# Low parts of x last in the first products of a sublayer, and three first tiles instead of two at five projections

## The chip, the cores and the metric

The kernel runs on one core of a Trainium2 chip. Its time is the device time of one execution, in microseconds; of several runs the median is taken. TensorE multiplies matrices, VectorE and GpSimd do elementwise work, ScalarE casts, squares and activations, SyncE issues most transfers.

## What is computed

Two blocks of a sequence model with 512 positions and 1024 channels, in fp32. The first has two layers, each of four sublayers, the second block three more:

```python
for l in range(DEPTH):
    x = x + 0.5 * rms_norm(swiglu(rms_norm(x, ln_ffn1_pre[l]), w_ffn1_in[l], w_ffn1_out[l]), ln_ffn1_post[l])
    mix = token_mixing(rms_norm(x, ln_mix_pre[l]), ...)
    x = x + rms_norm(mix, ln_mix_post[l])
    x = x + 0.5 * rms_norm(swiglu(rms_norm(x, ln_ffn2_pre[l]), w_ffn2_in[l], w_ffn2_out[l]), ln_ffn2_post[l])
    gate = jax.nn.sigmoid(rms_norm(x, ln_ple_pre[l]) @ w_ple_gate[l])
    x = x + rms_norm(gate * (p[l] @ w_ple_proj[l]), ln_ple_post[l])
x = x + hybrid_mixer(rmsnorm(x, norm_mix_w), ...)
x = x + memory_cross_attention(rmsnorm(x, norm_xattn_w), ...)
x = x + peer_ffn(rmsnorm(x, norm_ffn_w), ...)
```

So every sublayer norms x, projects it, and (in the first block) norms its result before adding it to x.

## The kernel before, in words

Activations lie with the channels on partitions: x is eight tiles of 128 channels by 512 positions. Every fp32 product is made of three: weights and activations are each split into a high part (rounded to the matmul's input type) and a low part (the rest), and `mm3` (line 196 is the matmul that it issues) adds high by high, weight high by x low, and weight low by x high. In the names of tiles `wh`, `wl` are the parts of a weight, `xh`, `xl` those of x, `st` the weight as loaded. `load_w` casts `st` to `wh` on ScalarE (line 186) and subtracts for `wl` on VectorE (line 187), in the last mixer (`mix2`) on GpSimd. There are three buffers each of `wh` and `wl`, two of `st`.

The norm's weight for a position is not applied to x but to the products: `bcast_R` adds up the squares (line 425), makes a reciprocal root in nine small steps on VectorE (lines 254 and 229 to 236, `rsm`, `rsy`, `rst`) and spreads it by TensorE and ScalarE to the tile R; the evacuations of the products multiply by R.

`lin_fm` makes a projection: for each output tile of 128 channels, three products for each of eight tiles of x. At a passage from one sublayer to the next the work is cut in two halves of 256 positions. The last `tail` output tiles of the old sublayer, and the first `head` tiles of the new one, run half by half. Between them stands `post_half`, once for each half: the old result's column sums (`ysum`, `ylast`, on TensorE into the bank `pr`), the nine steps, the multiply of each of eight tiles by R (line 347), the add of x (line 349 on VectorE for even tiles, line 348 on GpSimd for odd ones), the high part on ScalarE (line 351), the low part on VectorE (line 343), then squares for the new norm (lines 273 and 275). Its VectorE instructions are tied in the order written, and so are ScalarE's.

There are eight such passages: ffn to mixer, mixer to ffn, ffn to ple in both layers, ple to the next ffn, ple to the last mixer. The last mixer's output projection (`wdo`), the attention's two (`wxq`, `wxo`) and the last sublayer's (`wpq`) have heads without such a passage ahead; the first sublayer's x is split by `start`.

A scheduler orders each engine's queue ahead of time; `post_half`'s nine steps have a raised priority. Eight PSUM banks are named by use (`banks`); `hd` is the list for head tiles where one is given, otherwise the `ps` list.

## Time and profile before

| | us |
|---|---|
| median of 3 runs | 4402.1 |
| lowest, highest run | 4399.16, 4411.26 |
| profiled execution, its own time | 4405.5 |
| its span in the trace | 4403.7 |
| TensorE busy in it | 4137.3 |
| VectorE busy in it | 2627.9 |

The span runs from the first to the last instruction of the execution; what lies around it is the 1.8 us between the two. A busy TensorE is not TensorE at its peak, since its instructions overlap; where its pitch matters, the starts of its instructions are compared. The mean granted clock of the execution was 0.964 of 2.4 GHz.

### The profile page before, as it was taken

The numbers are of one execution on the slowest core, as the hardware profiler recorded it, in microseconds if no ns is written. First come the engines' busy times: TensorE is split into PE (matmuls) and PEld (weight loads), VectorE is DVE, ScalarE is ACT, GpSimd is POOL, SyncE is SP. The second block draws the span as 40 slices with busy tenths as digits, with TensorE's granted clock in tenths as the row PEclk, the third lists the DMA queues.
The fourth block names the chain that finished last, engine by engine and source line by source line (L and its number), as shares of the span: only waits on it lengthen the run. The fifth ranks groups of instructions, "written<-read, shape, count | busy, mean of one in ns | idle before, by whom it ended". The sixth has DMA issues, their size and how long they took to land. (4 is left out here: it accounts for less than half of the span.)

```text
span 4403.7 us, 56669 instructions
## 1 busy us (share of the span) xinstructions
PE 4137.3 (94%) x21835; PEld 3513.9 (80%) x21835; DVE 2627.9 (60%) x4873; ACT 1609.7 (37%) x2522; POOL 852.8 (19%) x755
## 2 busy tenths in 40 slices
PE   8999999999999999999999889899887889999998
PEld 7887687888888876878888677788777878888887
DVE  5435555643564345656434666636667878777876
ACT  3223423422443234324323543433334743333332
POOL 0002210100110012111001242104564124333331
PEclk9999989999999998989999899999898999999999
DMA  3233101323332341003223311435345689889985
GB/s 126 98 94 123 48 15 48 120 99 96 121 120 96 96 135 44 25 30 120 96 97 124 108 53 34 143 107 178 135 149 182 253 323 334 303 312 318 317 311 183
DMA packets 234815, 629.18 MB, mean 143 GB/s; under 512 B 26800, under 2 KB 93488, under 8 KB 230192
## 3 DMA queue, kind: packets, MB, share of 16 engines
q1 hardware_dynamic: 195232, 464.58, 30.8%
q0 software_dynamic: 38736, 159.93, 10.1%
q8 instruction: 171, 2.80, 0.2%
q10 hardware_dynamic: 576, 1.05, 0.1%
q14 instruction: 100, 0.82, 0.1%
HBM read 562.54 MB, written 62.91 MB: 142 GB/s over the span
## 5 line engine op out<-in xcount | busy, mean ns | idle before, releaser
L196 PE MATMUL ps_ps<-xh,wl 128*128 128x512 f32 (+2 forms) x3568 | 1307.3, 367 | 53.6 <-DVE wl L187 53.6
L196 PE MATMUL ps_ps<-xh,wh 128*128 128x512 f32 (+2 forms) x3568 | 1306.7, 368 | 32.6 <-ACT wh L186 11.9
L196 PE MATMUL ps_ps<-xl,wh 128*128 128x512 f32 (+2 forms) x3568 | 1314.2, 369 | 24.2 <-DVE xl L343 23.8
L186 ACT CAST wh<-st 128x1024 fp32r<-128x1024 f32 (+1 forms) x560 | 580.0, 1038 | 1405.2 <-PE ps_ps L196 962.3
L187 DVE TENSOR_TENSOR wl<-st,wh 128x1024 fp32r<-128x1024 f32 (+1 forms) x496 | 607.2, 1225 | 440.4 <-ACT wh L186 439.3
L196 PEld LDWEIGHTS ps_ps<-xh,wl 128*128 128x128 f32 x3568 | 689.0, 193 | 146.9 <-DVE wl L187 59.9
L196 PEld LDWEIGHTS ps_ps<-xl,wh 128*128 128x128 f32 x3568 | 688.1, 193 | 116.1 <-DVE xl L343 35.2
L196 PEld LDWEIGHTS ps_ps<-xh,wh 128*128 128x128 f32 x3568 | 686.4, 193 | 117.9 <-ACT wh L186 13.4
L442 DVE TENSOR_TENSOR gu<-ps_ps,R 128x512 f32<-128x512 f32 x176 | 121.0, 691 | 447.6 <-PE ps_ps L196 446.8
L348 POOL TENSOR_TENSOR y<-y,x 128x256 f32<-128x256 f32 x64 | 54.8, 856 | 1693.7 <-DVE y L347 1511.6
L196 PE MATMUL ps_ps<-mh,wl 128*128 128x512 f32 (+1 forms) x920 | 327.8, 356 | 2.5 <-DVE wl L187 2.5
L196 PE MATMUL ps_po<-vh,ah 128*128 128x512 f32 x768 | 303.2, 397 | 28.6 <-ACT ah L1845 21.8
L196 PE MATMUL ps_ps<-mh,wh 128*128 128x512 f32 (+1 forms) x920 | 327.4, 356 | 1.2 <-DVE kf L1518 0.9
L196 PE MATMUL ps_po<-vh,al 128*128 128x512 f32 x768 | 304.6, 397 | 4.5 <-DVE al L1846 4.4
L196 PE MATMUL ps_po<-vl,ah 128*128 128x512 f32 x768 | 303.2, 395 | 0.4 <-DVE vl L1852 0.4
L196 PE MATMUL ps_ps<-ml,wh 128*128 128x512 f32 (+1 forms) x792 | 289.4, 365 | 0.0
L187 POOL TENSOR_TENSOR wl<-st,wh 128x1024 fp32r<-128x1024 f32 x64 | 155.9, 2437 | 248.3 <-ACT wh L186 226.2
L1786 POOL DMA_INDIRECT rows<-in_pv_dram,idx x128 | 174.8, 1366 | 121.8 <-DVE acc L1809 114.1
L196 PEld LDWEIGHTS ps_ps<-mh,wl 128*128 128x128 f32 x920 | 174.9, 190 | 26.7 <-DVE wl L187 2.7
L196 PEld LDWEIGHTS ps_po<-vh,ah 128*128 128x128 f32 x768 | 146.4, 191 | 62.0 <-ACT ah L1845 26.2
L196 PEld LDWEIGHTS ps_ps<-mh,wh 128*128 128x128 f32 x920 | 174.8, 190 | 25.7 <-DVE kf L1518 1.1
L196 PEld LDWEIGHTS ps_po<-vh,al 128*128 128x128 f32 x768 | 146.1, 190 | 41.9 <-DVE al L1846 11.6
(699 smaller groups left out, 6047.2 us busy)
## 6 DMA issues: line engine op xcount, KB each, us to landing
st<-in_pu_dram SPq DMA_DIRECT2D x128, 512.0 KB
vst<-in_pv_dram SPq DMA_DIRECT2D x128, 512.0 KB
st<-in_w1i_dram SPq DMA_DIRECT2D x88, 512.0 KB
st<-in_w2i_dram SPq DMA_DIRECT2D x88, 512.0 KB
G<-gst POOLq DMA_DIRECT2D x12, 2048.0 KB
gt<-G SPq DMA_DIRECT2D x384, 64.0 KB
st<-in_wmf_dram SPq DMA_DIRECT2D x44, 512.0 KB
xd<-y SPq DMA_DIRECT2D x20, 1024.0 KB
```

The costliest lines, as they stand in the source:

```text
L186: nc.scalar.copy(out=wh[:, :n], in_=st[:, :n])
L187: self.wl_eng.tensor_sub(wl[:, :n], st[:, :n], wh[:, :n].bitcast(F32))
L196: i = self.nc.tensor.matmul(out, lhsT=lhsT, rhs=rhs, start=start, stop=stop)
L348: nc.gpsimd.tensor_add(y[k + 1], y[k + 1], self.xin[k + 1][:, c])
L442: nc.vector.tensor_mul(t, psum, R)
L1786: self.nc.gpsimd.indirect_dma_start(out=t, out_offset=None, in_=self.d["pur" if w == "u" else "pvr"], in_offset=bass.IndirectOffsetOnAxis( ...
```

## The change

Three things are changed. In `lin_fm` the head's products of a half are issued in three sweeps: all high by high, then all weight low by x high, then all weight high by x low; for `wdo` and `wxo` (`lows=False`) the three stay together for each tile of x, with the x low product last. In `post_half` two multiplies by R become one of 2 x 256 columns, and the eight low parts are issued behind all multiplies and adds. And five projections have three head tiles instead of two: the mixers' `wmf` (twice), the last mixer's `wdf`, and `wdo`, `wxq`, `wxo`. The banks are dealt out to match: a third bank for heads is taken from the attention's list in the mixers and from the gates' list in the last mixer, whose gates are now made with the third tile's evacuation instead of the first's.

```diff
@@ -343,17 +343,14 @@
             dve.append(nc.vector.scalar_tensor_tensor(l[:, c], y[k], self.v(next_gain, k), h[:, c].bitcast(F32), op0=ALU.mult, op1=ALU.subtract))
 
         for k in range(0, KD, 2):
-            for j in (k, k + 1):
-                dve.append(nc.vector.tensor_mul(y[j], y[j], R))
+            pair = self.yh[k // 4][:, k % 4:k % 4 + 2, c]
+            dve.append(nc.vector.tensor_mul(pair, pair, bc(R.unsqueeze(1), [P, 2, T // 2])))
             nc.gpsimd.tensor_add(y[k + 1], y[k + 1], self.xin[k + 1][:, c])
             dve.append(nc.vector.tensor_add(y[k], y[k], self.xin[k][:, c]))
             for j in (k, k + 1):
                 act.append(nc.scalar.activation(self.xs[j][0][:, c], y[j], AF.Copy, scale=self.v(next_gain, j)))
-            if k:
-                lo(k - 2)
-                lo(k - 1)
-        lo(KD - 2)
-        lo(KD - 1)
+        for k in range(KD):
+            lo(k)
         for i, j in zip(dve[1:], dve):
             self.behind(i, j)
         for i, j in zip(act[1:], act):
@@ -372,7 +369,7 @@
             self.yt = None
 
 
-    def lin_fm(self, wsrc, mts, xs, evac, tag, head=0, between=None, tail=0, done=None, wait=(2, 11)):
+    def lin_fm(self, wsrc, mts, xs, evac, tag, head=0, between=None, tail=0, done=None, wait=(2, 11), lows=True):
 
 
         kt = len(xs)
@@ -382,10 +379,12 @@
             pt = [self.ps([P, T], "hd" if "hd" in self.bank else tag) for _ in range(head)]
             ws = [load(m)[0] for m in mts[:head]]
             for c in HALVES:
-                for k in range(kt):
+
+                parts = ((0, 0), (1, 0), (0, 1))
+                steps = [(k, p) for p in parts for k in range(kt)] if lows else [(k, p) for k in range(kt) for p in parts]
+                for n, (k, (a, b)) in enumerate(steps):
                     for j in range(head):
-                        wh, wl, _, _ = ws[j]
-                        self.mm3(pt[j][:, c], (wh[:, k, :], wl[:, k, :]), (xs[k][0][:, c], xs[k][1][:, c]), k == 0, k == kt - 1)
+                        self.mm(pt[j][:, c], ws[j][a][:, k, :], xs[k][b][:, c], n == 0, n == len(steps) - 1)
             self.store_x()
             if between:
                 between()
@@ -552,7 +551,7 @@
         nc, tc, d = self.nc, self.tc, self.d
         with tc.tile_pool(name="mix", bufs=1, reuse_waits="tile") as pool:
             self.tags = {n: ("ax", AXB) for n in "rtab qk vat mq og".split()}
-            self.banks(ps=(0, 1), rw=(2, 3, 4), at=(5, 6, 7), pr=(6, 7))
+            self.banks(ps=(0, 1), rw=(2, 3, 4), at=(6, 7, 5), pr=(6, 7), hd=(0, 1, 5))
             self.pool, self.l = pool, l
             self.C = pool.tile([P, NC1], F32, name="C")
             nc.sync.dma_start(out=self.C, in_=d["C"])
@@ -587,7 +586,7 @@
                     for _ in range(2):
                         next(chain, None)
 
-            self.lin_fm(lambda m: [(d["wmf"][l][m], 0, KD)], list(range(16, 22)) + list(range(16)), self.xs, evac, "ps", head=2)
+            self.lin_fm(lambda m: [(d["wmf"][l][m], 0, KD)], list(range(16, 22)) + list(range(16)), self.xs, evac, "ps", head=3)
             for _ in att:
                 pass
             for _ in chain:
@@ -1196,7 +1195,7 @@
         nc, tc, d = self.nc, self.tc, self.d
         with tc.tile_pool(name="mx2", bufs=1, reuse_waits="tile") as pool:
             self.tags = {}
-            self.banks(ps=(0, 1), gi=(2, 3, 4), gn=(5,), gc=(6, 7), pr=(6, 7))
+            self.banks(ps=(0, 1), gi=(2, 3, 4), gn=(5,), gc=(6, 7), pr=(6, 7), hd=(0, 1, 4))
             self.pool = pool
             self.C = pool.tile([P, NC2], F32, name="C2")
             nc.sync.dma_start(out=self.C, in_=d["C2"])
@@ -1216,7 +1215,7 @@
                 nonlocal chain
                 if m < 12:
                     self.gd_tile(m, psum)
-                    if m == 0:
+                    if m == 2:
                         self.gd_gates()
                     if m == 11:
                         self.gd_core()
@@ -1231,7 +1230,7 @@
                         next(chain, None)
 
             self.wl_eng = nc.gpsimd
-            self.lin_fm(lambda m: [(d["wdf"][m], 0, KD)], list(range(24)), self.xs, evac, "ps", head=2)
+            self.lin_fm(lambda m: [(d["wdf"][m], 0, KD)], list(range(24)), self.xs, evac, "ps", head=3)
             self.wl_eng = nc.vector
             ys = []
             for q in range(2):
@@ -1244,7 +1243,8 @@
             for h in range(4):
                 self.split(self.gd[f"yg{h}"], *ys[4 + h])
             self.res_begin()
-            self.lin_fm(lambda m: [(d["wdo"][m], 0, KD)], list(range(KD)), ys, self.res_tile, "ps", head=2)
+            self.banks(ps=range(5), pr=(5, 6, 7))
+            self.lin_fm(lambda m: [(d["wdo"][m], 0, KD)], list(range(KD)), ys, self.res_tile, "ps", head=3, lows=False)
             self.res_end(next_gain)
 
     def lam_neg(self):
@@ -1558,7 +1558,7 @@
                 if m % 4 == 3:
                     scores(m // 4)
 
-            self.lin_fm(lambda m: [(d["wxq"][m], 0, KD)], list(range(KD)), self.xs, evac, "ps", head=2)
+            self.lin_fm(lambda m: [(d["wxq"][m], 0, KD)], list(range(KD)), self.xs, evac, "ps", head=3)
             ys = []
             for q in range(2):
                 h, lo = self.half(F32R, "ymh"), self.half(F32R, "yml")
@@ -1569,7 +1569,7 @@
                     self.mm(po, vt[:, kk, m * P:(m + 1) * P], pT[m // 2][:, kk, :], kk == 0, kk == 1)
                 self.split(po, *ys[m])
             self.res_begin()
-            self.lin_fm(lambda m: [(d["wxo"][m], 0, KD)], list(range(KD)), ys, self.res_tile, "ps", head=2)
+            self.lin_fm(lambda m: [(d["wxo"][m], 0, KD)], list(range(KD)), ys, self.res_tile, "ps", head=3, lows=False)
             self.res_end(next_gain)
 
 
```

Three places in the queues. VectorE at the first passage into a mixer, before: the second half of the nine steps of the second half's R, with what stands between and behind them up to the first multiply by R. `id` is a constant's cast, `ssum` an add of squares.

```order
L343 SCALAR_TENSOR_TENSOR xl<-y,V,xh 128x256
L234 SCALAR_TENSOR_TENSOR rst<-rsy 128x2
L343 SCALAR_TENSOR_TENSOR xl<-y,V,xh 128x256
L235 TENSOR_TENSOR rst<-rst,rsm 128x2
L343 SCALAR_TENSOR_TENSOR xl<-y,V,xh 128x256
L236 SCALAR_TENSOR_TENSOR rsy<-rst,rsy 128x2
L343 SCALAR_TENSOR_TENSOR xl<-y,V,xh 128x256
L275 TENSOR_TENSOR ssum_2632<-ssum_2632,sqx 128x256
L616 CAST id_2877<-io 128x128
L275 TENSOR_TENSOR ssum_2632<-ssum_2632,sqx 128x256
L347 TENSOR_TENSOR y<-y,ps_pr 128x256
```

And in the changed kernel, from the first half's low parts on, to the sixth of the nine steps (`wgl` is a gate weight's low part, line numbers behind line 349 are one lower or more):

```order
L343 SCALAR_TENSOR_TENSOR xl<-y,V,xh 128x256 x7
L254 TENSOR_SCALAR rsm<-ps_pr 128x2
L343 SCALAR_TENSOR_TENSOR xl<-y,V,xh 128x256
L229 TENSOR_SCALAR rsy<-rsm 128x2
L275 TENSOR_TENSOR ssum_2632<-ssum_2632,sqx 128x256
L230 TENSOR_TENSOR rst<-rsy 128x2
L187 TENSOR_TENSOR wl<-st,wh 128x1024
L231 TENSOR_TENSOR rst<-rst,rsm 128x2
L275 TENSOR_TENSOR ssum_2632<-ssum_2632,sqx 128x256
L232 SCALAR_TENSOR_TENSOR rst<-rst 128x2
L218 TENSOR_TENSOR wgl<-wg,wgh 128x64
L233 SCALAR_TENSOR_TENSOR rsy<-rst,rsy 128x2
```

All but one of the first half's low parts stand ahead of the first step, and a weight cast stands among the steps; before, the low parts stood between the steps.

TensorE at the same passage, before: the head's tenth to twelfth product of the first half, the column sums of the old result's second half, and the next products.

```order
L196 MATMUL ps_ps<-xh,wh 128x256
L196 MATMUL ps_ps<-xl,wh 128x256
L196 MATMUL ps_ps<-xh,wl 128x256
L196 MATMUL ps_pr<-io,ylast 128x1
L196 MATMUL ps_pr<-io,ysum 128x1
L196 MATMUL ps_pr<-io,ylast 128x1
L196 MATMUL ps_ps<-xh,wh 128x256 x2
L196 MATMUL ps_ps<-xl,wh 128x256
```

The changed kernel, from the head's first product on (`hd` is the bank list of heads):

```order
L196 MATMUL ps_hd<-xh,wh 128x256 x16
L196 MATMUL ps_hd<-xh,wl 128x256 x8
L196 MATMUL ps_pr<-io,ylast 128x1
L196 MATMUL ps_pr<-io,ysum 128x1
L196 MATMUL ps_pr<-io,ylast 128x1
L196 MATMUL ps_hd<-xh,wl 128x256 x8
L196 MATMUL ps_hd<-xl,wh 128x256 x3
L196 MATMUL ps_hd<-xh,wh 128x256 x8
L196 MATMUL ps_hd<-xl,wh 128x256 x3
L196 MATMUL ps_hd<-xh,wl 128x256 x8
L196 MATMUL ps_hd<-xl,wh 128x256 x2
L196 MATMUL ps_pr<-io,rsy 128x128 x2
```

The low parts of x come up first behind 32 products, the third tile's high products stand among theirs, and the column sums stand behind 24 products that need high parts alone; before, they stood behind twelve, four of which need a low part.

VectorE at the passage from ple into the last mixer, before: the end of the first half, with the evacuations of the old sublayer's last tiles (`gt`, `prj`) and the first step of the second half's R.

```order
L343 SCALAR_TENSOR_TENSOR xl<-y,V,xh 128x256 x2
L275 TENSOR_TENSOR ssum_18698<-ssum_18698,sqx 128x256
L343 SCALAR_TENSOR_TENSOR xl<-y,V,xh 128x256
L275 TENSOR_TENSOR ssum_18698<-ssum_18698,sqx 128x256
L343 SCALAR_TENSOR_TENSOR xl<-y,V,xh 128x256
L275 TENSOR_TENSOR ssum_18698<-ssum_18698,sqx 128x256
L486 TENSOR_TENSOR gt<-ps_ps,R 128x256
L489 TENSOR_TENSOR prj_18170<-prj_18170,gt 128x256
L486 TENSOR_TENSOR gt<-ps_ps,R 128x256
L322 TENSOR_TENSOR ysum<-ysum,sqy 128x256
L489 TENSOR_TENSOR prj_18171<-prj_18171,gt 128x256
L254 TENSOR_SCALAR rsm<-ps_pr 128x2
```

The changed kernel:

```order
L343 SCALAR_TENSOR_TENSOR xl<-y,V,xh 128x256 x8
L275 TENSOR_TENSOR ssum_18690<-ssum_18690,sqx 128x256 x2
L485 TENSOR_TENSOR gt<-ps_ps,R 128x256
L275 TENSOR_TENSOR ssum_18690<-ssum_18690,sqx 128x256
L488 TENSOR_TENSOR prj_18162<-prj_18162,gt 128x256
L485 TENSOR_TENSOR gt<-ps_ps,R 128x256
L322 TENSOR_TENSOR ysum<-ysum,sqy 128x256
L488 TENSOR_TENSOR prj_18163<-prj_18163,gt 128x256
L254 TENSOR_SCALAR rsm<-ps_pr 128x2
```

The evacuations and the step stand behind all eight low parts, as before; what stood between the low parts stands behind them.

## Rows read from the trace of the kernel before

**Rows 1.** Page: busy time by engine, and TensorE's busy tenths in 40 slices.
```profile
PE 4137.3 (94%) x21835; PEld 3513.9 (80%) x21835; DVE 2627.9 (60%) x4873; ACT 1609.7 (37%) x2522; POOL 852.8 (19%) x755
...
PE   8999999999999999999999889899887889999998
```
**Rows 2.** Windows of three passages: busy us of each engine, granted clock, DMA.
```profile
core 0: us, PE busy (x) PEld busy (x) DVE busy (x) ACT busy (x) POOL busy (x), PEclk, DMA share, GB/s
386.00:408.00 22.00, 17.48 (x109) 14.76 (x110) 20.86 (x52) 12.95 (x33) 13.06 (x16) 0.92 0.47 176
1233.30:1268.00 34.70, 26.65 (x176) 23.82 (x174) 28.14 (x70) 16.96 (x42) 10.90 (x13) 0.90 0.24 93
2468.40:2516.00 47.60, 33.01 (x156) 26.31 (x156) 37.89 (x85) 23.08 (x53) 23.09 (x21) 0.68 0.31 114
```
**Rows 3.** Waits of TensorE: us in total, times, longest.
```profile
PE ps_ps L196 <- DVE wl L187: 61.5, 17, 6.8
...
PE ps_ps L196 <- DVE xl L343: 23.8, 38, 2.4
```
**Rows 4.** Timeline of VectorE, first passage into a mixer: start, us, line, tiles.
```profile
384.33 1.76 DVE L187 TENSOR_TENSOR wl<-st,wh 128x1024 fp32r<-128x1024 f32 x1
...
393.24 0.68 DVE L236 SCALAR_TENSOR_TENSOR rsy<-rst,rsy 128x2 f32<-128x2 f32 x1
393.84 0.47 DVE L343 SCALAR_TENSOR_TENSOR xl<-y,V,xh 128x256 fp32r<-128x256 f32 x1
...
395.30 0.42 DVE L347 TENSOR_TENSOR y<-y,ps_pr 128x256 f32<-128x256 f32 x1 [0.18 <-PE ps_pr L196]
...
402.99 2.98 DVE L343 SCALAR_TENSOR_TENSOR xl<-y,V,xh 128x256 fp32r<-128x256 f32 x4
```
**Rows 5.** Timeline of VectorE, from ple into the last mixer.
```profile
2476.29 3.43 DVE L343 SCALAR_TENSOR_TENSOR xl<-y,V,xh 128x256 fp32r<-128x256 f32 x2
...
2488.09 0.16 DVE L254 TENSOR_SCALAR rsm<-ps_pr 128x2 f32<-128x2 f32 x1 [3.17 <-PE ps_pr L196]
...
2491.68 0.75 DVE L347 TENSOR_TENSOR y<-y,ps_pr 128x256 f32<-128x256 f32 x2 [1.38 <-PE ps_pr L196]
...
2492.69 0.75 DVE L347 TENSOR_TENSOR y<-y,ps_pr 128x256 f32<-128x256 f32 x2
...
2514.80 0.69 DVE L1262 TENSOR_TENSOR cx<-ps_ps,R 128x512 f32<-128x512 f32 x1 [2.87 <-ACT R L428]
```
**Rows 6.** Page: weight casts and low parts of weights; busy, mean ns of one.
```profile
L186 ACT CAST wh<-st 128x1024 fp32r<-128x1024 f32 (+1 forms) x560 | 580.0, 1038 | 1405.2 <-PE ps_ps L196 962.3
L187 DVE TENSOR_TENSOR wl<-st,wh 128x1024 fp32r<-128x1024 f32 (+1 forms) x496 | 607.2, 1225 | 440.4 <-ACT wh L186 439.3
...
L187 POOL TENSOR_TENSOR wl<-st,wh 128x1024 fp32r<-128x1024 f32 x64 | 155.9, 2437 | 248.3 <-ACT wh L186 226.2
```
**Rows 7.** Timeline of TensorE: head's last product and third tile's first, attention.
```profile
2893.95 0.28 PE L196 MATMUL ps_ps<-xh,wl 128*128 128x256 f32 x1
2894.07 0.40 PE L196 MATMUL ps_ps<-xh,wh 128*128 128x512 f32 x1
2894.30 0.40 PE L196 MATMUL ps_ps<-xl,wh 128*128 128x512 f32 x1
```
**Rows 8.** Timeline of TensorE: four waits, in brackets, at three passages and the start.
```profile
23.91 1.05 PE L196 MATMUL ps_pr<-io,ssum 128*128 128x1 f32 x8 [2.75 <-DVE ssum L425]
...
411.46 1.02 PE L196 MATMUL ps_pr<-io,ssum 128*128 128x1 f32 x8 [1.19 <-DVE ssum L425]
...
1267.90 0.79 PE L196 MATMUL ps_ps<-xh,wh 128*128 128x512 f32 x1 [0.30 <-ACT wh L186]
...
2494.26 0.80 PE L196 MATMUL ps_ps<-xh,wh 128*128 128x256 f32 x2 [2.61 <-ACT xh L351]
```
**Rows 9.** Timeline of VectorE: second half's first multiply or step, other passages.
```profile
801.02 0.75 DVE L347 TENSOR_TENSOR y<-y,ps_pr 128x256 f32<-128x256 f32 x2 [0.87 <-PE ps_pr L196]
...
1172.82 0.41 DVE L347 TENSOR_TENSOR y<-y,ps_pr 128x256 f32<-128x256 f32 x1
...
1250.25 0.16 DVE L254 TENSOR_SCALAR rsm<-ps_pr 128x2 f32<-128x2 f32 x1 [2.74 <-PE ps_pr L196]
```

## The prediction

> **What bounds the kernel now.** The page's first part comes first: TensorE is busy 94% of the span, VectorE 60%, and of 40 slices of the span most show TensorE at nine tenths or more [rows 1]. So over most of the kernel only TensorE time counts, and an edit can win only where TensorE stands still. The windows show where: at the passage from one sublayer to the next. In the 22 us around the first passage into a mixer TensorE is busy 17.48 us and VectorE 20.86; in the 47.6 us into the last mixer 33.01 and 37.89, at a mean granted clock of 0.68 of 2.4 GHz, that is, much of it at the lower level, 1.2 GHz [rows 2]. There, and only there, VectorE is the bound. The waits say for what TensorE stood: 23.8 us in 38 waits for the low part of x (line 343), 61.5 us in 17 for low parts of weights (line 187) [rows 3]. The last is the largest, and the change removes none of its causes.
>
> A passage has two halves of 256 columns. In each VectorE multiplies eight tiles by R and adds x, ScalarE makes the high parts, VectorE the low parts; the second half's R waits for the sum of squares of the last tile, made by nine small steps on VectorE. The kernel before puts the low parts between the sums, so a head product waits for a low part almost at once, while later high parts wait behind earlier low parts.
>
> **Part by part.** *The merged multiply.* Two multiplies by R in a row are 0.75 us [rows 4]; one of 512 columns from the same kind of operands took 0.69 [rows 5]. 0.06 x 4 pairs x 2 halves is 0.5 us a passage on VectorE, 4 us over the eight passages, and it is contained in the replays below.
>
> *The order of one half.* Sums of two tiles took 1.01 us, from 2491.68 to 2492.69 [rows 5]; 0.06 less, four times, is 3.8 us. Eight low parts at 0.47 each, undisturbed [rows 4], are as much. At the first passage into a mixer the second half's first multiply begins at 395.30 and the last four low parts at 402.99 for 2.98 us, so 10.7 us in all [rows 4]. I take 8.7 for the new order: 7.6 and 1.1 of stretching, since the adds of squares on GpSimd still run beside the low parts (the row with two low parts in 3.43 us beside a weight cast on GpSimd shows the worst of it [rows 5]; four in 2.98 the usual). The high parts of all tiles are there 5.5 us after the first multiply instead of about 8.5, and TensorE then has 48 products per three tiles that need no low part.
>
> *The price: the second half's R.* The nine steps stood between the first half's low parts, one by one. By the order above seven low parts now stand ahead of the first step, and a weight cast, two adds and small casts between the others. Replay: a weight cast on VectorE begins at 384.33 and took 1.76 us, 1.23 where nothing disturbs it [rows 4, 6]; two multiplies, three adds and two small steps behind it, 2.3 us, end the first half's sums at about 388.0; seven low parts bring 391.3, the nine steps at 0.2 are 1.8, what stands between them 2.8: 396.2. Before, the last step began at 393.24 and took 0.68 [rows 4], so 393.9. That half starts 2.3 us later: its first multiply at 397.1, its last low part at 405.8, against 406.0 before. VectorE ends the passage where it did.
>
> *Into the mixers of the two layers (2 passages).* Before, only some nine products of two tiles are left at the last low part, 406.0, 1.0 us of work. After, the 24 products with low parts begin when the 48 others are done, at about 405.9, and take 2.9 us; with the sums of squares between them 409.8, 2.8 us later than before, but with a third tile done in it: 48 products of 256 columns, 0.12 us apart, are 5.76 us, and the tile is then saved further on, at 24 products 0.23 us apart (two rows show each pitch [rows 7]), 5.45 us. The squares are added up earlier, which takes away most of the 1.19 us wait at 411.46 [rows 8]. 5.45 - 2.8 + 1.2 and up to 3 from an earlier R for the mixer's first tiles: I take 5 each (2 to 7), so 10 in both.
>
> *From mixer to ffn (2) and from ple to ffn (1).* Heads were three already. The second half's column sums stand behind first-half products on TensorE that waited for low parts; now these need high parts only, so R comes sooner: at the second its first step waited 2.74 us for TensorE, at 1250.25 [rows 9]. Replay: first multiply 1.9 us earlier than 801.02 in the first case, last low part 2.7 earlier, of which TensorE keeps 1.7, since the weight cast behind three tiles, 0.30 us of waiting before [rows 8], grows by 0.4: all products with the high weight now end last. Sum 3.5 for two (0 to 6). From ple the same gives 3 us earlier and 2.5 kept (0 to 4).
>
> *From ffn to ple (2).* The nine steps again fall behind seven low parts, and behind a weight cast and another; R comes 3.4 us later than the multiply at 1172.82 [rows 9] allowed, the shorter half gives 3 back. Sum 0 (-4 to 4 for two).
>
> *From ple to the last mixer (1).* The worst passage. Its second half's first step is at 2488.09, its first multiply at 2491.68 [rows 5], and TensorE waits 2.61 us for the high part up to 2494.26 [rows 8]. In the first half two low parts took 3.43 us beside a GpSimd weight cast [rows 5]; TensorE went at the half clock through products that low parts fed one by one. Replay: high parts 4 us earlier, first step at 2483, first multiply at 2486.5, heads (three now) done at 2502.4, the mixer's R first used at 2503.1 against 2514.80 [rows 5]. VectorE, which evacuates these tiles, is then 11.7 us earlier; TensorE gains the third tile's 5.45 besides, but waits for the evacuations. I take 11.5 (5 to 15).
>
> *Start (1).* The column sums of the first norm are asked of TensorE behind 55 products, not 73, and come from VectorE no sooner: it waited 2.75 us at 23.91 [rows 8], and 18 products at 0.12, 2.2 us, are now left behind that wait. -1.5 (-3 to 0).
>
> *The three other projections with a third tile.* Three weight buffers are then all in use. Before, the third weight was ready: at 2894.07 the third tile follows the second at pitch [rows 7]. After, the fourth tile's casts wait for the heads' last products: 1.04 us on ScalarE and 1.23 on VectorE [rows 6], of which three evacuations on other engines hide nothing; the third tile at half width costs 0.3 more. The row at 1267.90, where heads were already three, shows 0.30 us for the first cast [rows 8], because the first buffer comes free earlier than the last. Between 0.3 and 2.6: I take 1.7 for the two of the attention, and 1 for the mixer's output, where the products wait for the mixer itself. -4.4 (-7 to -1).
>
> Sum: 10 + 3.5 + 2.5 + 0 + 11.5 - 1.5 - 4.4 = 21.6 us. The profiled run is 4405.5 us, 3.4 above the median of 4402.1; from it 4383.9, from the median 4380.5. I say 4382. The low bounds add up to -5, the high ones to 42: 4407 to 4360.
>
> **A rule that speaks to the order.** Two low parts took 3.43 us in the row above while GpSimd ran a weight cast, and four 2.98 [rows 4, 5]; alone one takes 0.47. The Trainium skill, "GPSIMD Engine Reference", section "1. Specifications", says that GpSimd shares its SBUF interfaces with VectorE and contends with VectorE instructions that have two SBUF inputs. A low part has two such inputs, a multiply by R has one and one in PSUM; by that rule the sums suffer less, and low parts behind GpSimd's adds run alone. The trace agrees on the low parts. What it would be worth is worked out under the rivals.
>
> **Rivals.** *No measurable change.* VectorE is the bound at the passages (20.86 of 22 us [rows 2]) and has 0.5 us less to do in each; a half that ends where it ended and an R that comes later leave only the third tile, and the mixers may be paced by their evacuations so that a tile more at their start is waited away. Then the layers' mixers give 2 each, the last one 5, all else 0 except the losses: 4 + 5 - 5.9 = 3, about 4399. For it: the window's VectorE share. Against it: the slices after the first two passages into a mixer (the fifth to seventh and the sixteenth to eighteenth) have TensorE at nine tenths or more [rows 1].
>
> *Slower.* One mechanism: the three weight buffers. With all three held by heads, the next tile's weight starts at the heads' end, not ahead of it, at six places: two mixers, the last one, its output, two of attention. Each shows 1.04 + 1.23 us on VectorE, in the last mixer 1.04 + 2.44 on GpSimd [rows 6]. 5 x 2.3 + 3.5 is 15; with the 11 that the later R takes at four passages (2 x 2.3 and 2 x 3.4, kept in full) 26, against 12 that then remain of the gains: 4416. It decides if the buffers come free only with the last product of all heads, and the evacuations of three tiles come before the casts. Against it is the 0.30 us row.
>
> *More.* The low parts run alone at 0.47 behind the sums, and the stretches at the lower clock close. The first is 1.1 us x 8 passages, 9; the second, (1 - clock) x window, is 1.8, 3.5 and 15 us for the three windows [rows 2], of which I count 8 as lying beyond the sum. 9 + 8 on top of 21.6: 4364.
>
> That the change does not do what it says is excluded: the order shows each part of it.
>
> **How the numbers follow.** Forecast 4382 (between 4375 and 4389): 0.53. More, 4364: 0.15. No measurable change, 4399: 0.24. Slower, 4416: 0.08. A difference under 0.3%, 13.2 us, is about what a measurement of this kernel cannot tell from none. Faster by more than that (below 4388.9): the first two, 0.68. Within: 0.24. Slower: 0.08. The range leaves out the slower case and the outer half of the larger gain: 4360 to 4403.
>
> **What would show it.** In the profile after: waits of TensorE for the low part of x at line 343 well under 23.8 us; the second half's first multiply about 2 us later at 395 and 1173, earlier at 801, 1253 and by 5 at 2492; eight low parts in about 4.5 us; the last mixer's first evacuation some 11 us earlier; a new wait for the fourth weight of 1 to 2 us in the attention. It would be wrong if the mixers' length from their first evacuation to their end grew by what their start gained, or if the nine steps came later than replayed at the last mixer too.

## The result, and the profile after

The changed kernel took 4438.7 us (median of ten runs, 4424.1 to 4448.3), the kernel before 4402.1: 36.6 us apart; the ratio taken over the ten runs of each is 1.0075, with an interval of 1.0061 to 1.0090. The change made the kernel some 0.8% slower, where 20 us less was forecast. The profiled execution of the changed kernel took 4431.8 us, its span 4429.9; it lies 6.8 below its median, that of before 3.4 above, so the two traces show 26.2 of the 36.6 us.

What the change was to remove is nearly gone. In the page of the changed kernel the group of products with the low part of x (the last columns: idle before it, who ended most of it), and the one wait for it in the heads that have banks of their own (`hd`):

```profile
L196 PE MATMUL ps_ps<-xl,wh 128*128 128x512 f32 (+2 forms) x3456 | 1218.6, 369 | 0.3 <-DVE xl L343 0.3
...
PE ps_hd L196 <- DVE xl L343: 1.8, 1, 1.8
```

The waits of 23.8 us [rows 3] are 2.1. TensorE is also busier where it stood. The windows of the changed kernel over the three passages (the same times as before; columns as in [rows 2]):

```profile
386.00:408.00 22.00, 18.81 (x137) 16.78 (x137) 20.32 (x45) 13.04 (x33) 11.38 (x17) 1.00 0.50 176
1233.30:1268.00 34.70, 28.45 (x189) 26.51 (x188) 29.89 (x63) 18.29 (x44) 12.79 (x14) 0.85 0.29 107
2468.40:2516.00 47.60, 37.84 (x231) 34.93 (x230) 36.81 (x90) 23.12 (x54) 22.23 (x21) 0.78 0.28 101
```

The granted clock in the first and the third rose from 0.92 and 0.68 to 1.00 and 0.78, and TensorE's busy time from 17.48 to 18.81 and from 33.01 to 37.84 us; in the second the clock fell from 0.90 to 0.85. And still time was lost. The waits of TensorE in the changed kernel (us in total, times, longest) say on what, and two rows of the kernel before stand behind them:

```profile
PE ps_ps L196 <- DVE wl L187: 66.5, 18, 6.8
...
PE ps_ps L196 <- ACT wh L186: 19.6, 12, 8.4
PE ps_ps L196 <- ACT xh L351: 16.9, 18, 2.4
...
PE ps_hd L196 <- ACT xh L351: 10.3, 11, 2.7
...
PE ps_hd L196 <- DVE wl L187: 0.9, 2, 0.5
```

```profile
PE ps_ps L196 <- ACT wh L186: 12.1, 8, 8.0
PE ps_ps L196 <- ACT xh L351: 11.5, 6, 2.6
```

Before, the low parts of weights were 61.5 in 17 [rows 3], the high parts (`wh`) 12.1 in 8, the high parts of x 11.5 in 6. Against the 21.7 us taken away stand 15.7 more at the high parts of x and 13.4 more at the weights.

Where it was lost shows when the same instructions are looked for in both traces and their starts compared (minus is a loss, in us):

| stretch | bounded by | forecast | measured |
|---|---|---|---|
| start and first ffn | first product of the ffn's second projection | -1.5 | -4.5 |
| ffn into mixer, and mixer (2) | first product of the mixer's output | +10 | +13.1 |
| mixer into ffn (2) | first product of the ffn's second projection | +3.5 | -8.8 |
| ffn into ple (2) | first column sums of the ple's result | 0 | -4.0 |
| ple into ffn (1) | first product of the ffn's second projection | +2.5 | -1.7 |
| ple into the last mixer | its first evacuation | +11.5 | +4.2 |
| body of the last mixer | first product of its output | 0 | -13.6 |
| `wdo`, `wxq`, `wxo` | sums of squares of the last norm | -4.4 | -6.6 |
| last sublayer | end | 0 | -4.2 |

Three stretches make the result: the heads of the ffns, the body of the last mixer, and the start.

**The heads of an ffn.** From mixer to ffn, before, ScalarE, VectorE and TensorE (three timelines; times from the start, us):

```profile
814.97 2.00 ACT L186 CAST wh<-st 128x1024 fp32r<-128x1024 f32 x2 [4.76 <-PE ps_ps L196]
817.50 0.59 ACT L428 COPY R<-ps_pr 128x512 f32<-128x512 f32 x1 [0.53 <-PE ps_pr L196]
...
816.09 2.36 DVE L187 TENSOR_TENSOR wl<-st,wh 128x1024 fp32r<-128x1024 f32 x2
818.36 1.88 DVE L442 TENSOR_TENSOR gu<-ps_ps,R 128x512 f32<-128x512 f32 x3
...
816.07 0.49 PE L196 MATMUL ps_ps<-xh,wh 128*128 128x512 f32 x1 [0.31 <-ACT wh L186]
816.41 1.05 PE L196 MATMUL ps_pr<-io,rsy 128*128 128x128 f32 x8
```

And the changed kernel at the same place:

```profile
816.93 0.59 ACT L427 COPY R<-ps_pr 128x512 f32<-128x512 f32 x1 [8.29 <-PE ps_pr L196]
817.41 1.05 ACT L186 CAST wh<-st 128x1024 fp32r<-128x1024 f32 x1
...
817.55 1.89 DVE L441 TENSOR_TENSOR gu<-ps_ps,R 128x512 f32<-128x512 f32 x3 [1.87 <-ACT R L427]
819.35 1.22 DVE L187 TENSOR_TENSOR wl<-st,wh 128x1024 fp32r<-128x1024 f32 x1
...
812.88 1.02 PE L196 MATMUL ps_pr<-io,ssum 128*128 128x1 f32 x8 [1.45 <-DVE ssum L424]
...
815.74 1.16 PE L196 MATMUL ps_pr<-io,rsy 128*128 128x128 f32 x8
816.65 0.96 PE L196 MATMUL ps_ps<-xl,wh 128*128 128x256 f32 x6
818.51 0.50 PE L196 MATMUL ps_ps<-xh,wh 128*128 128x512 f32 x1 [0.91 <-ACT wh L186]
...
820.62 0.50 PE L196 MATMUL ps_ps<-xh,wl 128*128 128x512 f32 x1 [1.38 <-DVE wl L187]
```

Before, the casts of the fourth and fifth weight stand ahead of the copy of R on ScalarE and of the three evacuations (`gu`) on VectorE, and cover the time that R takes. After, all three high weights are held to the last of the head's products, the first cast stands behind the copy of R, its low part behind three evacuations. The first full-width product starts at 818.51, not at 816.07. That alone is no measure, since R's eight products (`rsy`), which followed it before, now stand ahead of the last six of the heads. Where both kernels have done the same, at the third full-width product, it is 820.62 against 817.53: 3.1 us later. Of these the longer wait for the high part is 0.6 and the new one for the low part 1.4; the column sums (`ssum`) wait 0.7 longer for VectorE (1.45 against 0.74), which is no matter of the weights.

**The body of the last mixer.** There the low parts of weights are GpSimd's. The evacuations by R (`cx`) and the steps behind them, changed kernel, VectorE, then ScalarE and GpSimd:

```profile
2516.51 0.69 DVE L1262 TENSOR_TENSOR cx<-ps_hd,R 128x512 f32<-128x512 f32 x1 [3.25 <-PE ps_hd L196]
2518.15 5.98 DVE L1171 SCALAR_TENSOR_TENSOR kf<-cx,V,kf 128x511 f32<-128x511 f32 x3 [0.95 <-ACT kf L1167]
...
2526.78 0.68 DVE L1262 TENSOR_TENSOR cx<-ps_hd,R 128x512 f32<-128x512 f32 x1
...
2537.83 2.43 DVE L1266 TENSOR_TENSOR kf<-kf,cx 128x512 f32<-128x512 f32 x1 [6.19 <-ACT cx L1265]
...
2536.22 1.05 ACT L186 CAST wh<-st 128x1024 fp32r<-128x1024 f32 x1 [6.95 <-issue]
...
2517.57 5.22 POOL L187 TENSOR_TENSOR wl<-st,wh 128x1024 fp32r<-128x1024 f32 x2 [8.88 <-ACT wh L186]
```

And before, GpSimd and VectorE:

```profile
2504.53 5.12 POOL L187 TENSOR_TENSOR wl<-st,wh 128x1024 fp32r<-128x1024 f32 x2 [0.66 <-ACT wh L186]
...
2516.29 2.32 DVE L1172 SCALAR_TENSOR_TENSOR kf<-cx,V,kf 128x511 f32<-128x511 f32 x3 [0.79 <-ACT kf L1168]
...
2521.25 0.68 DVE L1262 TENSOR_TENSOR cx<-ps_ps,R 128x512 f32<-128x512 f32 x1
```

Before, two weights were cast during the heads, ahead of the first evacuation. After, they come with it: the same three steps on `kf` take 5.98 us beside GpSimd's casts instead of 2.32, and 20 us further on a cast that stands 6.95 us on ScalarE keeps VectorE's next step waiting 6.19. The profile names no releaser for that cast, but its times do: the weight to be cast had landed by 2532.96, and the cast starts at 2536.22, right behind the end, at 2536.14, of TensorE's last product with the fourth tile's high weight. The times say that it waited for that weight's buffer. These products were late in turn: at 2526.91 TensorE had waited 3.56 us for a result that comes behind VectorE's stretched steps, and from 2527.6 to 2536.3 its granted clock was 0.50, the lower level, with products 0.43 us apart. The second evacuation comes 10.3 us behind the first instead of 6.5. VectorE's steps with two SBUF operands are slowed beside GpSimd's casts. The Trainium skill, "GPSIMD Engine Reference", section "1. Specifications", names such steps as those that contend with GpSimd; the trace agrees with 5.98 against 2.32.

### The profile page after: what moved, and what is told of

Same layout as the page of the kernel before. It is cut to its first block, busy times and chain, and to the rows that moved or that the text cites. A ratio compares the mean times of both kernels' runs of the same rounds, so it can differ in the third digit from the quotient of the medians.

```text
span 4429.9 us, 56925 instructions
## 1 busy us (share of the span) xinstructions
PE 4151.1 (94%) x21979; PEld 3534.1 (80%) x21979; DVE 2623.7 (59%) x4809; ACT 1607.6 (36%) x2522; POOL 860.9 (19%) x755
## 5 line engine op out<-in xcount | busy, mean ns | idle before, releaser
L196 PE MATMUL ps_ps<-xh,wh 128*128 128x512 f32 (+2 forms) x3456 | 1236.4, 372 | 44.2 <-ACT xh L351 16.9
L196 PE MATMUL ps_ps<-xh,wl 128*128 128x512 f32 (+2 forms) x3456 | 1217.8, 369 | 58.1 <-DVE wl L187 58.1
L196 PE MATMUL ps_ps<-xl,wh 128*128 128x512 f32 (+2 forms) x3456 | 1218.6, 369 | 0.3 <-DVE xl L343 0.3
L196 PEld LDWEIGHTS ps_ps<-xh,wl 128*128 128x128 f32 x3456 | 641.1, 193 | 148.7 <-DVE wl L187 64.6
L196 PEld LDWEIGHTS ps_ps<-xh,wh 128*128 128x128 f32 x3456 | 646.8, 193 | 138.4 <-ACT xh L351 26.1
L196 PEld LDWEIGHTS ps_ps<-xl,wh 128*128 128x128 f32 x3456 | 641.8, 193 | 80.5 <-issue 2.9
```

What stands on the lines that cost most here:

```text
L196: i = self.nc.tensor.matmul(out, lhsT=lhsT, rhs=rhs, start=start, stop=stop)
```

## The experiments

Medians are compared with runs of the kernel before on the same chip. One kernel's medians of ten and twelve runs differed by 12.5 us (the last section says where).

**Order or third tile?** Two theories stood first: (A) the new order costs, (B) the third tile costs. One run makes the new order with the old number of tiles and banks, the other the third tiles with the old order:

```diff
 e1: -  self.lin_fm(... d["wmf"] ..., head=3)      (and wdf, wdo, wxq, wxo, with the old banks)
     +  self.lin_fm(... d["wmf"] ..., head=2)
 e2: -  for k in range(KD): lo(k)                  (behind all sums)
     +  if k: lo(k - 2); lo(k - 1)                 (between them; the multiply of one tile; mm3 for each tile of x)
```

> The new order of products and of post_half alone, with two head tiles, banks and gates as before at the mixers, wdo, wxq, wxo (products at wdo and wxo as before). Theory A (the order is what costs: in the three sweeps the products with the high weight come last, so weight buffers and the norm's sums on TensorE's queue come late): the first ffn's first products some 4 us later, each other ffn 3 to 4, ple 1 to 2, so about +15 in all, 4415 to 4420; the last mixer's body is as long as before. Theory B (three heads are what costs, through the three weight buffers): 4400 to 4405, and the ffn's start where it was.

> Three head tiles at the five projections, with banks and gates as changed, but products and post_half in the order of before. Theory A: the layers' mixers gain 3 to 5 us each, the last mixer loses 10 to 14, wdo, wxq, wxo lose 5 to 8 together: 4405 to 4415. Theory B: all of the loss of the changed kernel, 4430 to 4440, with the ffn's start late too.

Measured: the order alone 4424.1, ratio 1.0052 (1.0035 to 1.0069); the tiles alone 4403.9, 1.0003 (0.9990 to 1.0017). So the order costs by itself, and the third tiles, by themselves, cost and give nothing that could be told. On top of the order they may cost the rest: the order alone lies 0.23% below the change, with intervals that overlap, and in its trace the last mixer's body lost 2.8 us and the three projections nothing, against 13.6 and 6.6 at the change.

**Which half of the order?**

```diff
 e5: sweeps of lin_fm as changed; post_half and heads as before
 e6: post_half as changed; lin_fm (mm3 for each tile of x) and heads as before
```

> The order of products (three sweeps) alone; post_half, heads, banks as before. Theory A1 (the sweeps cost: weights with the high part are used to the very end, the next tile's cast starts late, and more products stand behind the norm's sums on TensorE's queue): each ffn's first products 3 to 4 us later, 4412 to 4420. Theory A2 (post_half costs: the second half's R comes late because low parts stand ahead of its steps): 4400 to 4406.

> post_half with merged multiplies and the low parts behind all sums, alone; products in the order of before, where each tile's low part of x is asked for at once. Theory A1: 4402 to 4408, ffns start where they did. Theory A2: 4412 to 4420. Should both be near 4404, the two parts cost only together.

Measured: sweeps alone 4427.5, ratio 1.0050 (1.0029 to 1.0071); `post_half` alone 4442.8, 1.0096 (1.0069 to 1.0124). Each costs alone, and more than either expectation gave it: that one half would be free was wrong. For `post_half` the waits of TensorE say one reason:

```profile
PE ps_ps L196 <- DVE xl L343: 54.8, 17, 5.5
```

With the products still in the old order, the first of them meets a low part that is now made last: 54.8 us of waiting against 23.8 [rows 3]. The sweeps are the cure for that, and the sweeps have a price of their own.

But part of the price is the same in both. With `post_half` alone the weights still come free one after the other, and yet no cast stands ahead of the copy of R. ScalarE from mixer to ffn:

```profile
824.88 0.59 ACT L433 COPY R<-ps_pr 128x512 f32<-128x512 f32 x1 [8.26 <-PE ps_pr L196]
826.43 1.05 ACT L186 CAST wh<-st 128x1024 fp32r<-128x1024 f32 x1 [0.97 <-PE ps_ps L196]
```

R's products stand 20 products ahead of the heads' end there, so R is ready before a weight buffer is free; TensorE waits 0.30 for the high part and 1.41 for the low part. From the first evacuation of an ffn to its second projection `post_half` alone lost 4.0, 3.4 and 4.0 us, what the change lost. Over all runs with three buffers this goes by the place of the cast: where none stands ahead of the copy of R (the change, the order alone, the sweeps alone, `post_half` alone, and two runs below, that with two tiles in the last mixer and that with the smaller pool) each of these three stretches lost 3.4 to 5.6; where two do, none lost more than 1.7. So the sweeps are one way to a late cast, not the only one. The start, however, lost 4.3 with the sweeps alone and 0.6 with `post_half` alone.

**Is the price the late weight?** The changed kernel, but the last sweep of the second half goes tile by tile, so that the first two tiles' high weights come free earlier:

```diff
-                for n, (k, (a, b)) in enumerate(steps):
-                    for j in range(head):
-                        self.mm(...)
+                todo = [(n, k, p, j) for n, (k, p) in enumerate(steps) for j in range(head)]
+                if lows and c.start:
+                    todo = [t for t in todo if t[2] != (0, 1)] + sorted((t for t in todo if t[2] == (0, 1)), key=lambda t: t[3])
+                for n, k, (a, b), j in todo:
+                    self.mm(...)
```

> The changed kernel, but the last sweep of the second half goes tile by tile instead of by tiles of x, so that the first tile's high weight comes free 16 products (about 1.9 us) and the second's 8 products before the end. If the late release of the three weight buffers is what costs at the ffns and in the last mixer: 1 to 2 us back at each of four ffns, 3 to 10 in the last mixer, 4422 to 4432. If not: 4434 to 4440.

Measured 4402.6, ratio 0.9992 (0.9972 to 1.0012): by the ratios this one edit gave some 36 us back, where 7 to 17 were expected. ScalarE at the passage from mixer to ffn, with this edit:

```profile
821.87 2.00 ACT L186 CAST wh<-st 128x1024 fp32r<-128x1024 f32 x2 [5.89 <-PE ps_ps L196]
824.28 0.59 ACT L429 COPY R<-ps_pr 128x512 f32<-128x512 f32 x1 [0.41 <-PE ps_pr L196]
```

The two casts stand ahead of R again. From the first evacuation of an ffn to its second projection 4.0, 3.4 and 4.0 us were lost at the change, 0.8, 0.3 and 1.7 with the edit; the body of the last mixer lost 13.6, with the edit it won 0.3. TensorE's wait for the column sums (1.45) and R's products ahead of the last six of the heads are as in the change, so neither is what cost there.

But this edit moves products as well as buffers. So the wait was taken away with the order left as it is: a fourth buffer for a weight's high part, and two buffers fewer for small tiles to make the room; the kernel before with the same buffers beside it; and the changed kernel with the smaller pool alone:

```diff
-        wh = self.wst.tile([P, 1024], F32R, tag="wh", name="wh", bufs=HEAD)
+        wh = self.wst.tile([P, 1024], F32R, tag="wh", name="wh", bufs=4)
-        return self.tmpp.tile([P, T], F32, tag="tmp", name=name, bufs=12)
+        return self.tmpp.tile([P, T], F32, tag="tmp", name=name, bufs=10)
```

> The change as it is, with four buffers for the high part of a weight instead of three (and ten instead of twelve buffers for small tiles, which makes the room). Late release theory (the cost of the change is that three sweeps hold all three weight buffers to the end of the heads, so the next casts start late): the first of the two casts behind the heads finds a free buffer, the second does not; against the kernel before with the same buffers the change costs 5 to 22 us instead of 35; TensorE's first full width product behind the heads of the second ffn comes 0.5 to 1.5 us sooner than at the change, and the first evacuation of the last mixer's key tiles no longer waits 6 us for a cast. Rival (the sweeps' order of products costs by itself, or through ScalarE's and VectorE's queues, whatever the buffers are): 28 to 40 us above the kernel before with the same buffers.

> The kernel before with four buffers for the high part of a weight and ten for small tiles: the control of the run beside it. Late release theory: the old order gave a buffer back early, so a fourth is worth little: 4392 to 4406. Rival: the same.

> The change as it is, with three buffers for the high part of a weight as before and ten instead of twelve buffers for small tiles: the control that separates the two parts of the edit of the fourth buffer. Late release theory: the fourth buffer did it, so ten small tiles change nothing or cost a little: 4432 to 4448, and ScalarE's first cast behind the heads of the second ffn begins within 0.5 us of the end of the heads' products, not ahead of it. Rival (the smaller pool of small tiles changed the order of the queues, and that gave the 45 us): 4385 to 4410.

Measured: the change with four buffers 4393.2, ratio 0.9967 (0.9953 to 0.9981); the kernel before with four 4391.9, 0.9962 (0.9948 to 0.9977), at the fast edge of what was expected; the change with three and the smaller pool 4428.5, 1.0058 (1.0027 to 1.0090). With the fourth buffer the change costs 1.4 us where it cost 36.6, less than the 5 to 22 expected and not to be told from nothing; the smaller pool is not what did it. ScalarE, then TensorE, from mixer to ffn, change with four buffers:

```profile
809.65 1.05 ACT L186 CAST wh<-st 128x1024 fp32r<-128x1024 f32 x1 [7.54 <-PE ps_ps L196]
811.00 0.59 ACT L427 COPY R<-ps_pr 128x512 f32<-128x512 f32 x1 [0.31 <-PE ps_pr L196]
...
809.69 0.39 PE L196 MATMUL ps_ps<-xh,wl 128*128 128x512 f32 x1
```

The full-width products follow the heads with no wait at all (the fourth weight was cast during the heads), and the next cast stands ahead of R. With the smaller pool alone the order is that of the change, and the wait for the high part too (0.91):

```profile
822.57 0.59 ACT L427 COPY R<-ps_pr 128x512 f32<-128x512 f32 x1 [9.47 <-PE ps_pr L196]
823.06 1.05 ACT L186 CAST wh<-st 128x1024 fp32r<-128x1024 f32 x1
```

The first ffn lost 4.5 us at the change, at the order alone, at the sweeps alone and with the smaller pool (4.3 each), 0.5 with the tile-by-tile sweep, and won 0.8 with four buffers: the start's loss is the weights too. What four buffers do not cure is the last mixer. Its VectorE and GpSimd:

```profile
2484.51 5.97 DVE L1171 SCALAR_TENSOR_TENSOR kf<-cx,V,kf 128x511 f32<-128x511 f32 x3 [0.95 <-ACT kf L1167]
...
2483.93 5.22 POOL L187 TENSOR_TENSOR wl<-st,wh 128x1024 fp32r<-128x1024 f32 x2 [9.23 <-ACT wh L186]
```

Two casts still fall on the first evacuation, and its body still loses 8.5 us (the kernel before with four buffers 0.9). Nor is the third tile needed for this loss: with two tiles there, the sweeps alone lose 10.6 in this body and `post_half` alone 10.9. What the runs have in common is the second of GpSimd's two casts. Where it starts ahead of the first evacuation (before, and in every run that isn't named next) the body lost 3.8 at most; where it starts 0.4 to 1.0 us behind it (sweeps alone, `post_half` alone, three mixers with four buffers) it lost 10.6, 10.9 and 3.1, and where it starts 3.4 behind (the change, with four buffers, with the smaller pool) 13.6, 8.5 and 11.6. That the cast's place is the cause is likely, not shown: no run moved it alone.

**The last mixer and the three projections with a third tile.**

```diff
 e4: the change, with head=2, the old banks and the gates with the first evacuation in the last mixer
 e9: the tile-by-tile version, with head=2 at wdo, wxq and wxo
```

> The changed kernel with two head tiles, the old banks and the old place of the gates in the last mixer alone. If the third tile (weights of the fourth tile asked for only when the heads end) costs what the profile shows between the mixer's first evacuation and its output projection, 13.6 us: 10 to 15 us faster than the changed kernel, 4424 to 4428. If the order of products costs it: as slow as the changed kernel, 4436 to 4440.

> The changed kernel with the last sweep of the second half tile by tile, and two heads at wdo, wxq, wxo, banks there as before. From the profile with the tilewise sweep alone, the way from the last mixer's output projection to the sums ahead of the last sublayer is 4.5 us longer than before (2.6 at wdo, 3.0 at wxo, 1.2 shorter at wxq); theory: the third head there is what costs, so 4 to 5 us faster than that kernel, 4396 to 4400. If the third tile is not the cause there: 4401 to 4404.

Measured: 4433.5, ratio 1.0079 (1.0059 to 1.0100), and 4400.1, 0.9985 (0.9972 to 0.9998). In the first the last mixer's body loses 0.1 instead of 13.6, but its earlier stages, which the edit does not touch, came out some 7 us longer, so that the total tells nothing. In the second the stretch from `wdo` to the last norm wins 1.9 us where the version with three tiles loses 4.5; the totals, 2.5 apart, can't tell it.

**The order at the mixers alone.** The mixers are where the change won. There alone, first in the layers' two mixers, then tile by tile too, then the first again, and last with the last mixer (tile by tile in that one):

```diff
 e3, e11: new post_half where next_gain.startswith("mix_pre"); sweeps and head=3 at wmf alone; all else as before
 e8:      the same, the last sweep tile by tile
 e10:     new post_half where next_gain.startswith("mix"); sweeps and head=3 at wmf and wdf, tile by tile at wdf
 e14:     e10 with four buffers for wh and ten small tiles
```

> The new order and the third head tile only at the two passages into the layers' mixers; everything else as before. From the changed kernel's profile (the way from the sums of squares ahead of the mixer to its end was 5.4 and 7 us shorter there) theory A and B both expect 4388 to 4392. If the mixers' gain was only time lost earlier being made up, 4400 to 4403.

> The kernel with the new order and the third head only at the layers' mixers, with the last sweep tile by tile as well. By the release of buffers 1 to 2 us better at each mixer, 4387 to 4391; without an effect 4390 to 4394.

> The kernel with the new order and three heads at the layers' two mixers alone, once more, with more rounds: 4388 to 4394, a ratio to the kernel before of 0.996 to 0.999.

> New order of products and of post_half and three heads at the layers' two mixers and at the last one, there with the last sweep tile by tile; all other places as before. Theory (late release of the weight buffers is what cost in the last mixer): the last mixer from the sums ahead of it to its output projection is 2 us shorter than before, so 2 us better than with the layers' mixers alone, 4388 to 4392. If the later gates or the third tile cost there whatever the order, 8 to 12 us worse, about 4402.

> The kernel with the new order and three heads at the three mixers alone (the last one tile by tile in its last sweep), with four buffers for the high part of a weight. Late release theory: the two layers' mixers still hold all three buffers to the end of their heads, so a fourth gives 1 to 3 us at each: 4385 to 4396. Rival: no more than the control gains over the kernel before.

Measured: 4391.8, ratio 0.9986 (0.9970 to 1.0001); 4407.9, 1.0006 (0.9991 to 1.0021); 4404.3, 0.9992 (0.9982 to 1.0003); 4396.5, 0.9979 (0.9966 to 0.9991); with four buffers 4395.7, 0.9975 (0.9957 to 0.9992). The first and the third are the same kernel, 12.5 us apart in their medians, and each interval holds 1: the gain of the layers' mixers is best put at some 0.1%, and can't be told from none. That the first of them fell into its expected 4388 to 4392 was luck; its repeat and the tile-by-tile version missed theirs. With the last mixer it is faster than the kernel before by 0.2%; there the way from the ple's last column sums to the output's first product is 5.9 us shorter. The lowest ratio of all is that of the old order with a fourth buffer and the smaller pool, 0.4% below the kernel before; the change with the same buffers can't be told from it.

## Why the prediction was wrong

**Right.** The waits for low parts of x fell from 23.8 to 2.1. The layers' mixers gave 13.1 against a forecast of 10, though part of that is the clock (last section). The second half's R came later by as much as replayed where it was replayed with care: at the first mixer its first multiply is at 402.03 against 395.30 [rows 4], 2.2 later beside the 4.5 that the whole stretch is late (forecast 2.3); at the ple 1178.50 against 1172.82 [rows 9], 2.5 beside 3.2 (forecast 3.4). Two sums of that replay don't come out as written: 391.3, 1.8 and 2.8 make 395.9, not 396.2, and 2.3 behind 395.30 is 397.6, not 397.1. They are small beside what follows. The order of both kernels, read before, was what ran.

**Wrong: "the weight cast behind three tiles, 0.30 us of waiting before, grows by 0.4".** It grew to 0.91 for the high part and 1.38 for the low part, and the third full-width product starts 3.1 us later. Forecast +3.5 for two such passages, measured -8.8. The row of 0.30 us [rows 8] is the price of the *old* queues, in which the casts stand ahead of the copy of R; it was carried over to a change that moves them behind it. And the price was taken for the wait of one engine: what stands between the cast and its users changed on ScalarE (the copy of R) and on VectorE (three evacuations). The queues are ordered ahead of time, so this could have been read in them without a run: the two casts ahead of the copy before, behind it after. Making the weights come free together is not the whole of it, since `post_half` alone moves the casts too.

**Wrong: the place of the rival.** The slower case named the late weight buffers, with their deciding point ("the evacuations of three tiles come before the casts"), and gave it 8 in 100, since it was looked for only at the six places that get a third tile. It decides at heads that had three tiles already, and at the start: 4.5 + 4.1 + 4.7 + 1.7 is 15 us, none of it in the rival's list. What the projections with a new third tile lost, 6.6 against 4.4, lies inside its range.

**Wrong: "I take 8.7 for the new order".** A half takes as long as before. VectorE of the changed kernel, second half of the first passage into a mixer:

```profile
402.03 0.69 DVE L347 TENSOR_TENSOR y<-y,ps_pr 128x512 f32<-128x512 f32 x1 [0.80 <-PE ps_pr L196]
...
403.10 0.68 DVE L347 TENSOR_TENSOR y<-y,ps_pr 128x512 f32<-128x512 f32 x1
...
406.47 0.59 DVE L275 TENSOR_TENSOR ssum<-ssum,sqx 128x256 f32<-128x256 f32 x1 [0.58 <-ACT sqx L273]
...
407.32 5.41 DVE L343 SCALAR_TENSOR_TENSOR xl<-y,V,xh 128x256 fp32r<-128x256 f32 x8
```

From 402.03 to 412.73 are 10.7 us, what it was before. The sums of two tiles start 1.07 apart, not 0.95 (before 1.01 [rows 5]): the merged multiply saved nothing here. An add of squares that waits 0.58 for ScalarE stands ahead of the last sum, and the eight low parts take 5.41, not 4.9 (4.70 at the next passage). So each earlier second half that the replays drew lost 2 us of its ground: at 801.02 [rows 9] the multiply was forecast 1.9 earlier and came 0.95 later (801.09, in a kernel that stood 0.88 ahead at the mixer's output).

**Wrong: "first step at 2483" at the last mixer.** It came at 2493.72, waiting 3.28 us for TensorE, which counted from the ple's first column sums, themselves 5.9 later, is where it was. TensorE ahead of it, and the step on VectorE:

```profile
2486.24 0.58 PE L196 MATMUL ps_hd<-xl,wh 128*128 128x256 f32 x1 [1.80 <-DVE xl L343]
2486.61 3.85 PE L196 MATMUL ps_hd<-xh,wh 128*128 128x256 f32 x16
...
2491.12 0.42 PE L196 MATMUL ps_pr<-io,ysum 128*128 128x1 f32 x2
...
2493.72 0.16 DVE L254 TENSOR_SCALAR rsm<-ps_pr 128x2 f32<-128x2 f32 x1 [3.28 <-PE ps_pr L196]
```

The column sums still stand behind a low part, one of the first half, for which TensorE waits 1.80; and they stand behind more products, a third tile's among them, which go at 0.24 us apiece, twice the pitch of [rows 7]. The granted clock was 0.62 in the 18 us up to 2494, most of it the lower level, as in the like stretch before. The 11.5 forecast came out as 4.2, and the body, which was held to be unchanged, lost 13.6.

**The sum.** As they ran, the gains are 13.1 in the layers' mixers and 4.2 on the way into the last one; against them stand the start with 4.5, the heads of the three later ffns with 10.5, the two ple with 4.0, the last mixer's body with 13.6, the three projections with 6.6 and the last sublayer with 4.2: 26 us lost. The start and the ffns are the late weights: with four buffers they no longer lose. Each ple wins 4 with them, of which the kernel before with four buffers wins 2 as well. The last mixer's body is cured by the tile-by-tile sweep and only in part by the buffer, so its cause is in part open, as said above. The last sublayer ran between 6.5 us shorter (the tile-by-tile version) and 9.4 longer (three mixers with four buffers) without a pattern in the edits; what sets it was not tried, nor was the fourth buffer in the old order without the smaller pool beside it. Nor was a cast put ahead of the copy of R with three buffers and all else as changed, which would part the place in the queue from the free buffer.

## What to carry to other kernels

When products are put in another order, ask first what the order releases: an operand's last use sets when its buffer is loaded again, and sweeps over all tiles move every last use to the end. Ask next what else becomes ready before that, for it takes the place in the queue of the engine that refills the buffer: here the copy of R, moved ahead of the weight casts by the sweeps and by the later low parts alike. A wait read in the old order prices the old order; what it becomes must be read from the new queues, of the engine that refills the buffer and of the one behind it, and one buffer more is the quickest test. Here that buffer, with the smaller pool beside it, gave 0.4% in the old order, and the reordering on top of it gave nothing that could be told.

## What the runs showed of the hardware

TensorE's clock in the layers' mixers. These are stretches of the layers' second mixer, with TensorE's busy time, granted clock and DMA. The first two rows are its earlier half in two executions of one kernel, that with the order at the layers' mixers alone; the third is a part of its later half in that kernel with the tile-by-tile sweep:

```profile
1640.10:1806.10 166.00, 156.71 (x832) 0.96 0.13 47
...
1646.00:1819.00 173.00, 164.21 (x832) 0.91 0.13 45
...
1903.00:1928.00 25.00, 25.00 (x81) 0.52 0.06 22
```

The same 832 instructions take 166 or 173 us, at a mean granted clock of 0.96 or 0.91; and TensorE is recorded as busy in 25.00 of 25.00 us at 0.52, that is, near the lower level of 1.2 GHz throughout, with 81 instructions in them. So a stretch without a recorded pause is no warrant of the higher level, and the time at the lower one differs between two executions of one kernel: this half mixer took 7 us more in one. The two executions are 19.9 us apart in all; some 10 of these lie in the layers' two mixers, and 7 in the last sublayer, where the granted clock is 0.95 in both. That is the spread in which the mixers' own gain could not be told from none.

Three steps of VectorE with two SBUF tiles each took 5.98 us beside casts on GpSimd, 2.32 without them. The casts themselves took 2.41 and 2.85 there, and 2.34 to 2.38 further on in the same body. In the kernel before, the two casts took 2.36 and 2.80, with an add of VectorE beside each: these adds took 2.73 and 2.31, the second on 128x4 elements, where the like one behind it took 0.16.
